# Both output projections of the mixer and of the cross attention in seven products of half-size blocks, their weight operands prepared and stored during the first FFN

## The chip, the core and the metric

The kernel runs on one core of a Trainium2 chip. TensorE multiplies matrices into PSUM, VectorE and ScalarE work element by element, GpSimd does small steps, and SyncE (SP in the profile) issues the DMAs. Each engine runs its own instructions in order; semaphores order them between engines. The time is device microseconds of one execution, the median of several runs.

## The reference

A decoder layer on x with T = 1024 tokens and D = 1024 features, in fp32:

```python
h = _layer_norm(ALPHA * h + 0.5 * _swiglu(h, ffn1_w_gate, ffn1_w_up, ffn1_w_down), ln1_g, ln1_b)
mix = _token_mixers(h, w_in, ..., w_out)             # concat([o_a, o_b]) @ w_out
h = _layer_norm(ALPHA * h + mix, ln2_g, ln2_b)
xa = _memory_cross_attention(h, mem, ..., xa_w_o)    # o.reshape(T, D) @ xa_w_o
h = _layer_norm(ALPHA * h + xa, ln3_g, ln3_b)
h = _layer_norm(ALPHA * h + 0.5 * _swiglu(h, ffn2_w_gate, ffn2_w_up, ffn2_w_down), ln4_g, ln4_b)
```

The FFNs have 2816 hidden features. The mixers are a gated linear recurrence with 4 heads of 128 (its normed and gated output is o_a, 512 features) and a spatial gating unit (o_b, 512 features). The cross attention has 4 heads of 256 and 256 memory tokens. The two products with w_out and xa_w_o, each 1024 x 1024 x 1024, are the output projections spoken of here.

## The kernel before

**Products.** Every fp32 operand is split into two fp32r tiles, hi = a rounded copy (ScalarE, L109) and lo = the operand less hi (VectorE, L110). `mm3` (L130) then makes one product of three matmuls, hi hi (L131), lo hi (L132) and hi lo (L133), each 128x128 by 128x512 into one PSUM bank. Activations are kept transposed (feature by token) in the tiles xh and xl, two halves of 512 tokens each, in eight k-tiles of 128 features.

**Stages.** In order: FFN 1; the mixers, first half of the tokens, then the second; the first output projection with LN2 (names acc_mx, wd_mx, r_mx); the cross attention, whose query projection (paq, weights waq) takes the normed tokens; the second output projection with LN3 (acc_xa, wd_xa, r_xa); FFN 2. The FFNs already use Winograd's form of Strassen's product, seven products of half-size blocks where the plain way has eight: gate and up (st_gf, st_uf) over 11 pairs of feature tiles, 7 products of 12 matmuls for each, and the down projection (dp_f).

**An output projection** is `down_group` (L226), called for the groups of token tiles (0, 1), (2, 3, 4) and (5, 6, 7). For every group the eight row blocks of the weights are loaded (512 KB each, SP's queue), split, and multiplied with the group's tiles, two PSUM banks a tile: 8 x 8 x 2 x 3 = 384 matmuls over the three groups, and 24 loads with 24 splits. Behind each group `residual_norm` (L214) runs for each of its tiles as a coroutine: it loads the residual, adds the accumulators on VectorE (L220), normalizes (L191 to L204), stores, and after a lag transposes the tile on TensorE (L158) back into xh and xl.

**What sets the order.** Coroutines are started with `spawn`, and `tick(us)` lets them go on when so many us of matrix products have been issued since. Tiles come from pools: `gpool` with 22 tiles of 4 KB a partition, `wpool` with 3 raw, 6 hi and 5 lo tiles for weights, and PSUM with 6 banks for products and 2 for transposes. A tile waits until the last reader of the buffer it takes has finished, and an engine that waits holds up what stands behind it on the same engine; SP issues all DMAs here, so a load that waits for a buffer holds up the loads and stores behind it. In the mixers `m1.tail()` is the last part of the second half: its four gate products (ps_wg, 48 matmuls each) and, by coroutine, the gating and the transposes of o (pt_oa). Group (0, 1) of the first projection, tokens of the first half, is run ahead of it (its residuals and norms fall into it), the other groups behind it. The query projection then starts with half 0, and the groups of the second projection run in the same manner, the first one inside the loop over the heads of half 1. FFN 2 starts with its first pair of feature tiles (pg_f).

Of the kernel before, what the change touches and what calls it, by code (L numbers as in the profile page):

```python
# [33 lines left out]
def hybrid_layer_kernel(ctx: ExitStack, tc: tile.TileContext, a, out):  # L34
# [29 lines left out]
    # Work that follows a matrix product on other engines runs as a coroutine: where the tensor  # L64
    # engine would wait for it, it yields the time of other products (in us) to issue first.
# [26 lines left out]
    # the tensor engine's clock rises while it works: transposes until the first tile is there  # L92
# [9 lines left out]
    # left and right operands of the products of the FFNs' down projection, by pair of feature tiles  # L102
    lops = dram.tile([7, NF // 2, P, HALF], F32, name="lops")
    rops = dram.tile([2, NF // 2, P, HALF], F32, name="rops")
    res = [dram.tile([T, D], F32, name=f"res{i}") for i in range(3)]

# [23 lines left out]
    def mm3(ps, lh, ll, rh, rl, first, last):  # L130
        nc.tensor.matmul(ps, lh, rh, start=first, stop=False)  # L131
        nc.tensor.matmul(ps, lh, rl, start=False, stop=False)  # L132
        nc.tensor.matmul(ps, ll, rh, start=False, stop=last)  # L133
# [73 lines left out]
    def layer_norm(y, gb, bb, name):  # L207
        """y: [P, 1024] tile, normalized over its free dim in place."""
# [5 lines left out]
    def residual_norm(tt, lag, acc, res_src, gb, bb, dst, name, keep=None):  # L214
        """dst = LN(alpha * res_src + acc) for a token tile, and its transpose."""
        r = gt(f"r_{name}")
        nc.sync.dma_start(r, res_src[tt * P:(tt + 1) * P, :])
        for dh in range(2):
            sl = slice(dh * 512, (dh + 1) * 512)
            nc.vector.scalar_tensor_tensor(r[:, sl], r[:, sl], ALPHA, acc[dh], op0=ALU.mult, op1=ALU.add)  # L220
        layer_norm(r, gb, bb, name)
        nc.sync.dma_start(dst[tt * P:(tt + 1) * P, :], r)
        yield lag
        yield from to_xT_steps(r, tt, list(range(KT)), name, keep, 2.6)
# [982 lines left out]
```

## Time and profile before

| | |
|---|---|
| Time, median of 3 runs (lowest, highest) | 2041.24 us (2035.83, 2042.89) |
| Span of the profiled execution | 2032.8 us |
| First and last start of st_gf (FFN 1 and FFN 2 together) | 62.7 and 1780.4 us |
| Gate products of the mixers (ps_wg), last start | 1082.5 us |
| First output projection (acc_mx), first and last start | 1022.2 and 1152.6 us |
| Query projection (paq), first and last start | 1152.8 and 1265.4 us |
| Second output projection (acc_xa), first and last start | 1275.2 and 1386.2 us |
| First gate product of FFN 2 (pg_f), start | 1386.5 us |

All but the first row are of one profiled execution, whose span is a little shorter than the time of the runs. Names are those of the tiles; a matmul counted as 0.39 us in the profile overlaps the next one. The profile's rows on which the argument rests are shown in the prediction, beside what is read from them.

### The profile page before, as it was taken

The page shows a single profiled execution, that of the slowest core. Times are in us where ns is not written, and L with a number is a line of the kernel's source. Part 1 is how long each engine was busy: PE and PEld are TensorE (multiplying, and loading weights), DVE is VectorE, ACT ScalarE, POOL GpSimd, SP SyncE. Part 2 cuts the span into 40 slices and gives each one's busy share as a digit, 9 for nine tenths or more (in the row PEclk, how much of TensorE's full clock was granted, in tenths as well). Part 3 has the DMA queues.
Part 4 walks back from the last instruction along what each step waited for, and adds up shares of the span by engine and source line. Part 5 has one row for each costly group of instructions (what it writes and reads, how often), then busy time and mean ns, then how long its engine had stood idle before and what let it go on. Part 6 is the DMA issues. An engine that isn't in the chain of part 4 may idle for free.

```text
span 2032.8 us, 25339 instructions
## 1 busy us (share of the span) xinstructions
PE 2015.5 (99%) x9646; PEld 1689.1 (83%) x9646; DVE 1504.1 (74%) x2246; ACT 890.0 (44%) x1239; POOL 102.5 (5%) x144
## 2 busy tenths in 40 slices
PE   8999999999999999999999999999999999999998
PEld 7888888888888888888888888888888888888886
DVE  5987677677668967948796855678776776776688
ACT  6633333334533467547644344444333333344432
POOL 0000000000002010100110100010000000000021
PEclk8999999999999999999999999999999999999999
DMA  8333233237887632123156522353232332378874
GB/s 263 122 114 119 78 114 119 78 119 250 290 289 261 222 116 73 53 63 105 41 176 228 162 88 74 122 197 119 88 126 82 104 127 81 109 249 291 297 254 172
DMA packets 244250, 306.88 MB, mean 151 GB/s; under 512 B 14368, under 2 KB 154272, under 8 KB 244128
## 3 DMA queue, kind: packets, MB, share of 16 engines
q1 hardware_dynamic: 244128, 305.26, 45.3%
q8 instruction: 76, 1.25, 0.2%
q14 instruction: 46, 0.38, 0.1%
HBM read 234.44 MB, written 70.78 MB: 150 GB/s over the span
## 4 chain that ended last, share of the span: by engine, by line
PE 93%; DVE 3%; DMA 2%; POOL 1%; issue 1%; SPq 0%; ACT 0%; POOLq 0%; DVEq 0%; ACTq 0%
PE st_gf L131 7%; PE st_uf L131 7%; PE st_gf L133 7%; PE st_uf L133 7%; PE st_gf L132 7%; PE st_uf L132 7%; PE dp_f L133 6%; PE dp_f L131 6%; PE dp_f L132 6%; PE psl L939 2%; PE acc_xa L131 1%; PE acc_xa L133 1%; PE acc_xa L132 1%; PE paq L131 1%; PE paq L133 1%; PE paq L132 1%
## 5 line engine op out<-in xcount | busy, mean ns | idle before, releaser
L132 PE MATMUL dp_f<-wd_f_l,ah_f 128*128 128x512 f32 x552 | 213.3, 390 | 0.0
L131 PE MATMUL dp_f<-wd_f_h,ah_f 128*128 128x512 f32 x552 | 208.4, 390 | 0.0
L133 PE MATMUL dp_f<-wd_f_h,al_f 128*128 128x512 f32 x552 | 206.1, 390 | 0.1
L133 PEld LDWEIGHTS dp_f<-wd_f_h,al_f 128*128 128x128 f32 x552 | 103.7, 188 | 22.2 <-DVE al_f L110 0.9
L132 PEld LDWEIGHTS dp_f<-wd_f_l,ah_f 128*128 128x128 f32 x552 | 103.6, 188 | 21.6
L131 PEld LDWEIGHTS dp_f<-wd_f_h,ah_f 128*128 128x128 f32 x552 | 103.6, 188 | 21.2
L109 ACT ACTIVATE wd_f_h<-wd_f_r 128x1024 fp32r<-128x1024 f32 x72 | 73.2, 1022 | 97.7 <-DVE wd_f_r L436 28.3
L110 DVE TENSOR_TENSOR al_f<-ar_f,ah_f 128x1024 fp32r<-128x1024 f32 x72 | 84.5, 1174 | 24.5 <-ACT ah_f L109 23.6
L109 ACT ACTIVATE ah_f<-ar_f 128x1024 fp32r<-128x1024 f32 x72 | 73.3, 1019 | 59.2 <-DMA ar_f<-lops 54.3
L110 DVE TENSOR_TENSOR wd_f_l<-wd_f_r,wd_f_h 128x1024 fp32r<-128x1024 f32 x72 | 84.3, 1175 | 12.5 <-ACT wd_f_h L109 12.2
L316 DVE TENSOR_TENSOR top_uf<-bot_uf,st_uf 128x512 f32<-128x512 f32 x21 | 14.4, 686 | 81.8 <-PE st_uf L133 81.8
L315 ACT ACTIVATE bot_gf<-st_gf 128x512 f32<-128x512 f32 x21 | 12.5, 597 | 137.1 <-PE st_gf L133 137.1
L560 POOL TENSOR_SCALAR nm_f<-nm_f 128x1 f32<-128x1 f32 x8 | 10.7, 1336 | 1198.8 <-ACT xl L559 1198.8
L131 PE MATMUL st_gf<-xh,wg_f_h 128*128 128x512 f32 x168 | 65.4, 389 | 0.0
L133 PE MATMUL st_gf<-xh,wg_f_l 128*128 128x512 f32 x168 | 65.4, 389 | 0.0
L131 PE MATMUL st_uf<-xh,wu_f_h 128*128 128x512 f32 x168 | 65.4, 389 | 0.0
L132 PE MATMUL st_uf<-xl,wu_f_h 128*128 128x512 f32 x168 | 65.4, 389 | 0.0
L133 PE MATMUL st_uf<-xh,wu_f_l 128*128 128x512 f32 x168 | 65.4, 389 | 0.0
L132 PE MATMUL st_gf<-xl,wg_f_h 128*128 128x512 f32 x168 | 65.3, 389 | 0.0
L109 ACT ACTIVATE wg_f_h<-wg_f_r 128x1024 fp32r<-128x1024 f32 x44 | 46.4, 1056 | 36.2 <-PE st_gf L132 29.3
L109 ACT ACTIVATE wu_f_h<-wu_f_r 128x1024 fp32r<-128x1024 f32 x44 | 46.3, 1053 | 35.7 <-issue 27.2
L110 DVE TENSOR_TENSOR wu_f_l<-wu_f_r,wu_f_h 128x1024 fp32r<-128x1024 f32 x44 | 53.6, 1219 | 3.2 <-PE acc_xa L132 3.2
(456 smaller groups left out, 5960.1 us busy)
## 6 DMA issues: line engine op xcount, KB each, us to landing
ar_f<-lops SPq DMA_DIRECT2D x66, 512.0 KB, 5.0
wd_f_r<-in_ffn_w_down_dram SPq DMA_DIRECT2D x56, 512.0 KB, 4.8
wg_f_r<-in_ffn_w_gate_dram SPq DMA_DIRECT2D x44, 512.0 KB, 3.8
wu_f_r<-in_ffn_w_up_dram SPq DMA_DIRECT2D x44, 512.0 KB, 3.8
wd_mx_r<-in_w_out_dram SPq DMA_DIRECT2D x24, 512.0 KB, 3.6
wd_xa_r<-in_xa_w_o_dram SPq DMA_DIRECT2D x24, 512.0 KB, 3.5
lops<-bot_gf SPq DMA_DIRECT2D x21, 512.0 KB, 2.7
lops<-top_uf SPq DMA_DIRECT2D x21, 512.0 KB, 2.8
```

The lines of the kernel that those rows point to most:

```text
L109: order(nc.scalar.activation(hi, src, AF.Copy))
L110: order(nc.vector.tensor_tensor(lo, src, hi.bitcast(F32), op=ALU.subtract))
L131: nc.tensor.matmul(ps, lh, rh, start=first, stop=False)
L132: nc.tensor.matmul(ps, lh, rl, start=False, stop=False)
L133: nc.tensor.matmul(ps, ll, rh, start=False, stop=last)
L315: nc.scalar.activation(b0, product(1), AF.Copy)
L316: nc.vector.tensor_tensor(t0, b0, product(2), op=ALU.add)
L560: nc.gpsimd.tensor_scalar(nmean, nmean, -1.0 / D, None, op0=ALU.mult)
L939: nc.tensor.matmul(psl[:m, (i * NC2 + c) * 64:(i * NC2 + c + 1) * 64] .rearrange("p (n b) -> p n b", b=B), e[:, :m], blk(e, B)[:, :, 1, :] ...
```

## The change

Both projections are made of seven products in Winograd's form. The tokens (two halves), the 1024 features (two halves) and the output columns (two halves) form 2x2 blocks. A product is four token tiles by 512 columns, 4 k-tiles and three matmuls: 48 matmuls, so 7 x 48 = 336 for a projection.

**Weight operands.** The seven right operands of each projection are blocks of the weights and running sums of them. They are made once, in FFN 1, by the coroutine `prepare_square`, a step each 13 us of products, 28 steps in all (7 operands x 2 pairs of k-tiles x 2 projections). A step loads a block into the one tile `pre`, or adds a block to what is there with an accumulating DMA that GpSimd issues (16 of the 28); ScalarE makes hi and -hi; a second accumulating DMA adds the block to -hi, which gives lo; both are stored to DRAM (hi from SP, lo from GpSimd). `later` starts the coroutine behind the memory keys and values. The projections load their operands ready (`fetch`, sh and sl, 28 loads of 512 KB for each projection) and split nothing.

**Token operands.** These need differences of the attention or mixer outputs of the two halves. The transposed outputs of the first half are stored (oa, ao) and loaded again (mx_again, ao_again); VectorE subtracts, and the results take the places of xh and xl.

**Order.** The first projection has its products in the order 2, 1 (ahead of `m1.tail()`), then behind it 7, 4, 6, 5 and 3. Product 5 completes the tokens of half 1 (done5), product 3 those of half 0 (done3); the tokens of half 1 take their LN statistics on ScalarE and GpSimd, those of half 0 on VectorE. The query projection starts with half 1. The second projection runs 1 and 7 inside the loop over the heads of half 0, then 4, 6, 5, 2, 3.

The core of the diff (comments that it drops, and helpers that only rename, are left out):

```diff
...
+    SUMS = {1: ["11"], 5: ["11", "12"], 6: ["11", "12", "22"], 4: ["11", "12", "22", "21"],
+            2: ["21"], 3: ["22"], 7: ["22", "12"]}
+    def prepare_square(w, ops, name):
+        wv = w.rearrange("(kb n i p) (db d) -> kb n db p i d", kb=2, n=2, i=2, p=P, db=2)
+        for n in range(2):
+            raw = None
+            for p, blocks in SUMS.items():
+                b = wv[int(blocks[-1][0]) - 1, n, int(blocks[-1][1]) - 1]
+                if len(blocks) == 1:
+                    raw = wpool.tile([P, 2, HALF], F32, tag="pre", bufs=1, name=f"pre_{name}_{n}{p}")
+                    nc.sync.dma_start(raw, b)
+                else:
+                    nc.gpsimd.dma_start(raw, b, accum_op=ALU.add)
+                hi = wpool.tile([P, 2, HALF], F32R, tag="whi", bufs=6, name=f"ph_{name}_{n}{p}")
+                lo = wpool.tile([P, 2, HALF], F32R, tag="wlo", bufs=5, name=f"pl_{name}_{n}{p}")
+                nc.scalar.activation(hi, raw, AF.Copy)
+                nc.scalar.activation(lo, hi.bitcast(F32), AF.Copy, scale=-1.0)
+                nc.gpsimd.dma_start(lo, raw, accum_op=ALU.add)
+                nc.sync.dma_start(ops[p - 1, n, 0], hi.bitcast(F32))
+                nc.gpsimd.dma_start(ops[p - 1, n, 1], lo.bitcast(F32))
+                yield 13
+    class Square:
...
+        def fetch(self, *ps):
+            for p in ps:
+                self.right[p] = []
+                for n in range(2):
+                    hi = wpool.tile([P, 2, HALF], F32R, tag="whi", bufs=6, name=f"sh_{self.name}_{p}{n}")
+                    lo = wpool.tile([P, 2, HALF], F32R, tag="wlo", bufs=5, name=f"sl_{self.name}_{p}{n}")
+                    for i, t in enumerate((hi, lo)):
+                        nc.sync.dma_start(t.bitcast(F32), self.ops[p - 1, n, i])
+                    self.right[p].append((hi, lo))
...
+        def part(self, p, bank, half, k0, t, n, first):
+            ts = slice(t * P, (t + 1) * P)
+            rh, rl = self.right[p][n]
+            for i in range(2):
+                k = k0 + 2 * n + i
+                mm3(bank[t], xh[half][:, k, ts], xl[half][:, k, ts], rh[:, i, :], rl[:, i, :],
+                    first and n == 0 and i == 0, n == 1 and i == 1, not first)
+        def step(self, p, bank, half, k0, n, first=False):
+            for t in range(4):
+                self.part(p, bank, half, k0, t, n, first)
+            tick(5.4)
+        def tiles(self, p, bank, half, k0, done, first=False):
+            for t in range(4):
+                for n in range(2):
+                    self.part(p, bank, half, k0, t, n, first)
+                done(t)
+                tick(2.7)
...
+        def finish(self, x, p2=None):
+            f, g = self.f, self.g
+            self.fetch(6)
+            for t in range(4):
+                self.residual(self.bot, g, t)
+                self.onto(self.bot[t][:, 1], x[t], ALU.subtract, ALPHA)
+            self.step(4, x, g, 4, 0)
+            self.step(4, x, g, 4, 1)
+            s1, s4 = {}, {}
+            for n in range(2):
+                self.put(self.s[n], f, 0, n)
+            for n in range(2):
+                s1[n] = self.a1[0][n]
+                nc.vector.tensor_tensor(s1[n], s1[n], self.s[n], op=ALU.subtract)
+                self.put(s1[n], g, 0, n)
+            self.fetch(5)
+            for t in range(4):
+                self.onto(self.bot[t][:, 0], x[t], ALU.add, ALPHA)
+            y = self.bank("sy")
+            def done6(t):
+                self.onto(self.bot[t][:, 0], y[t], ALU.subtract)
+            self.tiles(6, y, f, 0, done6, True)
+            for n in range(2):
+                s4[n] = self.a1[1](n)
+                nc.vector.tensor_tensor(s4[n], s4[n], self.s[n], op=ALU.subtract)
+                self.put(s4[n], f, 0, n)
+            self.fetch(3)
+            self.junk = gt("junk_xa") if p2 is None else xl[f][:, 4:6, :].rearrange("p k t -> p (k t)")
+            def done5(t):
+                self.onto(self.bot[t][:, 1], y[t])
+                self.early.append(self.norm(self.bot[t], g, t, 8 + 2.5 * t))
+                spawn(self.early[-1])
+            self.tiles(5, y, g, 0, done5)
+            if p2 is None:
+                self.fetch(2)
+            for t in range(4):
+                if p2 is None:
+                    self.residual(self.top, f, t)
+                    self.onto(self.top[t][:, 0], self.p1[t], ALU.add, ALPHA)
+                    self.onto(self.top[t][:, 1], self.p1[t], ALU.subtract, ALPHA)
+            if p2 is None:
+                z = self.bank("sz")
+                def done2(t):
+                    self.onto(self.top[t][:, 0], z[t])
+                self.tiles(2, z, f, 4, done2, True)
+            def done3(t):
+                self.onto(self.top[t][:, 1], y[t])
+                spawn(self.norm(self.top[t], f, t, 8 + 2.5 * t))
+            self.tiles(3, y, f, 0, done3)
...
+        spawn(later())
+    def later():
+        yield 20
+        for n, w in (("mx", a["w_out"][0]), ("xa", a["xa_w_o"][0])):
+            yield from prepare_square(w, sq_ops[n], n)
...
-            to_xT(o, self.half * NC2 + i, [0, 1, 2, 3], f"oa{self.half}{i}")
...
+            if self.half:
+                for n in range(2):
+                    if i == 0:
+                        msq.s[n] = gt(f"s3_mx{n}", (P, 2, HALF))
+                        msq.a1[0][n] = mixed_again(0, n)
+                    nc.vector.tensor_tensor(msq.s[n][:, :, cs], msq.a1[0][n][:, :, cs],
+                                            ptv[:, 2 * n:2 * n + 2, :], op=ALU.subtract)
+                    if last:
+                        msq.put(msq.s[n], 1, 0, n)
+                        msq.put(self.u[n], 1, 4, n)
+                        nc.vector.tensor_tensor(msq.s[n], msq.s[n], self.u[n], op=ALU.add)
+                return
...
+                    nc.sync.dma_start(oa_dram[0, j], self.oa[j])
...
+    def mixed_again(j, n):
+        t = gt(f"mx_again{j}{n}", (P, 2, HALF))
+        nc.sync.dma_start(t, oa_dram[j, n])
+        return t
...
-    run(mix_group((0, 1)))
+    msq.fetch(2, 1)
+    x = msq.bank("sx2")
+    for n in range(2):
+        msq.step(2, x, 0, 4, n, True)
+    msq.p2 = msq.copies(x, "p2")
+    x = msq.bank("sx")
+    for n in range(2):
+        msq.step(1, x, 0, 0, n, True)
     play(m1.tail())
+    msq.fetch(7)
+    msq.gb, msq.bb = load_bc(a["ln2_g"][0], a["ln2_b"][0], "mx")
+    for t in range(4):
+        msq.residual(msq.top, 0, t)
+        msq.onto(msq.top[t][:, 0], msq.p2[t], ALU.add, ALPHA)
+        msq.onto(msq.top[t][:, 0], x[t])
+        msq.onto(msq.top[t][:, 1], x[t], ALU.subtract, ALPHA)
     drain()
-    run(mix_group((2, 3, 4)))
-    run(mix_group((5, 6, 7)))
-    # ---- cross attention ----
+    for n in range(2):
+        msq.step(7, x, 1, 0, n)
+    msq.fetch(4)
+    msq.finish(x, msq.p2)
+    F, G = 1, 0
...
-        q_proj(0, c)
+        q_proj(F, c)
...
+    sq.fetch(1)
+    x = sq.bank("sx")
     for h in range(H):
-        if h:
-            next(first)
-        probs_T(1, h)
+        probs_T(G, h)
+        if h == 0:
+            sq.a1[0].update({n: attended_again(n) for n in range(2)})
         if h < H - 1:
-            scores(1, h + 1)
+            scores(G, h + 1)
+        if h < 2:
+            sq.step(1, x, F, 0, h, True)
+        elif h == 2:
+            sq.p1 = sq.copies(x, "p1")
+            sq.step(7, x, G, 0, 0)
         else:
-            next(first)
-        next(first)
-        attend(1, h)
-    run(first)
-    run(out_group((2, 3, 4)))
-    run(out_group((5, 6, 7)))
-    # ---- FFN 2 ----
+            sq.step(7, x, G, 0, 1)
+        if h == 1:
+            sq.fetch(7)
+        if h == 2:
+            sq.fetch(4)
+            sq.gb, sq.bb = load_bc(a["ln3_g"][0], a["ln3_b"][0], "xa")
+        attend(G, h)
+    sq.finish(x)
```

Three places show how it moves instructions.

**TensorE behind the last gate product** of the mixers (ps_wg_3; pt_oa are the transposes of o; wd_mx, sh_mx and sl_mx are weight operands; sy_mx are the banks of product 6, sx_mx those of products 1, 7 and 4). Before, the engine has there:

```order
L132 MATMUL ps_wg_3_8737<-wg_l,xh_116 128x512
L133 MATMUL ps_wg_3_8737<-wg_h,xl_118 128x512
L131 MATMUL acc_mx_0_8797<-wd_mx_0_h,xh_115 128x512
L132 MATMUL acc_mx_0_8797<-wd_mx_0_l,xh_115 128x512
L133 MATMUL acc_mx_0_8797<-wd_mx_0_h,xl_117 128x512
L131 MATMUL acc_mx_1_8798<-wd_mx_0_h,xh_115 128x512
L132 MATMUL acc_mx_1_8798<-wd_mx_0_l,xh_115 128x512
L133 MATMUL acc_mx_1_8798<-wd_mx_0_h,xl_117 128x512
L131 MATMUL acc_mx_0_8799<-wd_mx_0_h,xh_115 128x512
L158 MATMUL pt_oa_0_8765<-ident,ot_7748 128x128 x4
L158 MATMUL pt_oa_0_8772<-ident,ot_7748 128x128 x4
L132 MATMUL acc_mx_0_8799<-wd_mx_0_l,xh_115 128x512
```

Now it has, from the last rows of the same gate product:

```order
L136 MATMUL ps_wg_3_8905<-wg_l,xh_116 128x512
L137 MATMUL ps_wg_3_8905<-wg_h,xl_118 128x512
L1038 MATMUL pt_oa_8933<-ident,ot_8002 128x128 x4
L1038 MATMUL pt_oa_8946<-ident,ot_8002 128x128 x4
L1038 MATMUL pt_oa_8953<-ident,ot_8005 128x128 x4
L1038 MATMUL pt_oa_8992<-ident,ot_8005 128x128 x4
L135 MATMUL sy_mx_9155<-sh_mx_9065,xh_115 128x512
L136 MATMUL sy_mx_9155<-sl_mx_9066,xh_115 128x512
L135 MATMUL sy_mx_9156<-sh_mx_9065,xh_115 128x512
L136 MATMUL sy_mx_9156<-sl_mx_9066,xh_115 128x512
L135 MATMUL sx_mx_8680<-sh_mx_8960,xh_116 128x512
L136 MATMUL sx_mx_8680<-sl_mx_8961,xh_116 128x512
```

The matmuls of the group (2, 3, 4) that stood between the last gate product and the transposes are gone: all four transposes follow at once, and behind them the first rows of products 6 and 7, whose token operands are made from them.

**SP's queue there.** oa is the stored output of the first half, res the residual, sq_mx the prepared operands. Before, from the last weights of the first group on:

```order
L118 DMA wd_mx_7_r<-in_w_out_dram 128x1024
L118 DMA wg_r<-in_w_in_dram 128x2x512 x3
L217 DMA r_mx_8538<-res_121 128x1024
L217 DMA r_mx_8554<-res_121 128x1024
L118 DMA wg_r<-in_w_in_dram 128x2x512
L118 DMA wd_mx_0_r<-in_w_out_dram 128x1024
L118 DMA wd_mx_1_r<-in_w_out_dram 128x1024
L118 DMA wd_mx_2_r<-in_w_out_dram 128x1024
L118 DMA wd_mx_3_r<-in_w_out_dram 128x1024
```

Now, from the operands of product 4 on (9065 to 9069 are product 6's):

```order
L268 DMA sh_mx_9057<-sq_mx 128x1024
L268 DMA sl_mx_9058<-sq_mx 128x1024
L268 DMA sh_mx_9061<-sq_mx 128x1024
L268 DMA sl_mx_9062<-sq_mx 128x1024
L268 DMA sh_mx_9065<-sq_mx 128x1024
L268 DMA sl_mx_9066<-sq_mx 128x1024
L1231 DMA mx_again_8939<-oa 128x1024
L268 DMA sh_mx_9069<-sq_mx 128x1024
L1231 DMA mx_again_8943<-oa 128x1024
L191 DMA g_mx<-in_ln_g_dram 128x1024
L192 DMA b_mx<-in_ln_b_dram 128x1024
L298 DMA r_mx<-res_125 128x1024 x8
```

The two loads of mx_again are now in a row with the loads of operands, behind most of them, and the residuals (r_mx) stand behind both.

**VectorE at the end of the first projection**, up to the query projection (xl is the lo part of the transposed tokens, 117 of half 0 and 118 of half 1; pt_mx are the transposes on TensorE; r_mx the tiles being normed; waq the query weights). Before, at the place where the first query weights are split:

```order
L110 TENSOR_TENSOR xl_117<-pt_mx_0_9097,xh_115 128x4x128
L110 TENSOR_TENSOR xl_117<-pt_mx_4_9128,xh_115 128x4x128
L202 SCALAR_TENSOR_TENSOR r_mx_9027<-r_mx_9027,mv_mx_9034,g_mx 128x1024
L110 TENSOR_TENSOR waq_0_l<-waq_0_r,waq_0_h 128x1024
L204 SCALAR_TENSOR_TENSOR r_mx_9027<-r_mx_9027,rs_mx_9036,b_mx 128x1024
L110 TENSOR_TENSOR waq_1_l<-waq_1_r,waq_1_h 128x1024
L110 TENSOR_TENSOR xl_117<-pt_mx_0_9135,xh_115 128x4x128
L110 TENSOR_TENSOR xl_117<-pt_mx_4_9166,xh_115 128x4x128
L110 TENSOR_TENSOR waq_2_l<-waq_2_r,waq_2_h 128x1024
L110 TENSOR_TENSOR xl_118<-pt_mx_0_9173,xh_116 128x4x128
L110 TENSOR_TENSOR xl_118<-pt_mx_4_9204,xh_116 128x4x128
L110 TENSOR_TENSOR waq_3_l<-waq_3_r,waq_3_h 128x1024
```

Now, from the addition of product 3's last bank on:

```order
L302 TENSOR_TENSOR r_mx<-r_mx,sy_mx_9158 128x512
L200 BN_AGGR mv_mx_9359<-st_mx_9356 128x2
L113 TENSOR_TENSOR xl_118<-pt_mx_0_9368,xh_116 128x4x128
L113 TENSOR_TENSOR xl_118<-pt_mx_4_9400,xh_116 128x4x128
L206 SCALAR_TENSOR_TENSOR r_mx<-r_mx,mv_mx_9359,g_mx 128x1024
L196 BN_STATS st_mx_9388<-r_mx 128x6 x2
L113 TENSOR_TENSOR xl_118<-pt_mx_0_9432,xh_116 128x4x128
L208 SCALAR_TENSOR_TENSOR r_mx<-r_mx,rs_mx_9361,b_mx 128x1024
L200 BN_AGGR mv_mx_9391<-st_mx_9388 128x2
L206 SCALAR_TENSOR_TENSOR r_mx<-r_mx,mv_mx_9391,g_mx 128x1024
L196 BN_STATS st_mx_9420<-r_mx 128x6 x2
L208 SCALAR_TENSOR_TENSOR r_mx<-r_mx,rs_mx_9393,b_mx 128x1024
```

The splits of the transposed tokens, which alternated with query weights and the last rows of the group before, now alternate with the scalings and statistics of the other half's tiles, and the query weights stand ahead of them.

More of the change, by code (lines that the diff above doesn't have):

```diff
@@ L212, in layer_norm @@
         ln_apply(y, stt, gb, bb, name)
[L214 to L224, printed above, removed]
@@ L1124, in attend @@
         pTh, pTl = pts[half, h]
+        n = h % 2
+        if half == F:
+            ao = gt(f"ao{h}", (P, 2, HALF))
+        elif h < 2:
+            sq.s[n] = gt(f"s3_xa{n}", (P, 2, HALF))
         for j in range(2):
```

140 lines of the change are left out of this document (98 added, 42 removed).

## The prediction

> **What bounds the kernel now.** First the page: its span, and the engine that fills it.
>
> ```profile
> span 2032.8 us, 25339 instructions
> PE 2015.5 (99%) x9646; PEld 1689.1 (83%) x9646; DVE 1504.1 (74%) x2246; ACT 890.0 (44%) x1239; POOL 102.5 (5%) x144
> GB/s 263 122 114 119 78 114 119 78 119 250 290 289 261 222 116 73 53 63 105 41 176 228 162 88 74 122 197 119 88 126 82 104 127 81 109 249 291 297 254 172
> ```
>
> Then the waits of TensorE (total us, times, longest), longest and last of those that matter here:
>
> ```profile
> PE ptm L660 <- ACT mem L653: 3.3, 2, 2.2
> ...
> PE psl L939 <- DVE r_mx L220: 0.4, 1, 0.4
> ```
>
> Then busy time by stretch (sum and count for PE, PEld, DVE, ACT, POOL; granted clock, DMA share, GB/s): the start, first FFN, first output projection, second one.
>
> ```profile
> 10.00:15.00 5.00, 2.56 (x12) 1.86 (x12) 3.27 (x4) 2.99 (x4) 0.00 (x0) 0.64 1.08 380
> 15.00:20.00 5.00, 4.46 (x21) 4.26 (x21) 3.60 (x8) 2.21 (x3) 0.00 (x0) 0.50 1.07 366
> 20.00:25.00 5.00, 5.00 (x37) 5.00 (x36) 2.92 (x5) 0.63 (x1) 0.00 (x0) 0.83 1.12 317
> 200.00:250.00 50.00, 50.00 (x223) 41.39 (x222) 33.27 (x44) 16.09 (x20) 0.00 (x0) 1.00 0.28 90
> 1050.00:1100.00 50.00, 49.58 (x275) 42.61 (x275) 37.09 (x57) 21.69 (x42) 5.88 (x8) 1.00 0.53 197
> 1100.00:1150.00 50.00, 50.00 (x234) 41.58 (x233) 38.39 (x45) 20.95 (x23) 5.40 (x6) 1.00 0.60 196
> 1350.00:1400.00 50.00, 50.00 (x238) 41.56 (x237) 42.86 (x61) 18.77 (x38) 10.01 (x12) 1.00 0.54 182
> ```
>
> TensorE is the bound: after the start it waits 0.4 us in all. So matrix work that is removed is time gained, and every wait that is added on TensorE is time lost. Note VectorE in the stretches of the projections: 37 to 43 of 50 us. It has little room for a burst.
>
> **What is removed.** 50 us hold 222 to 223 matmuls of 512 columns; rows follow each other by 0.227 us (timeline: start, length, row), eight transposes take 0.8:
>
> ```profile
> 1093.15 0.39 PE L132 MATMUL acc_mx<-wd_mx_l,xh 128*128 128x512 f32 x1
> 1093.38 0.40 PE L133 MATMUL acc_mx<-wd_mx_h,xl 128*128 128x512 f32 x1
> 1093.61 1.04 PE L158 MATMUL pt_oa<-ident,ot 128*128 128x128 f32 x8
> 1094.40 0.70 PE L133 MATMUL acc_mx<-wd_mx_h,xl 128*128 128x512 f32 x2
> ```
>
> Each projection goes from 384 to 7 x 48 = 336 matmuls: 2 x 48 x 0.227 = **21.8 us gained**. One product (48) is 10.9 us, one of its four tiles 2.7. That 48 splits on ScalarE and VectorE go too is worth nothing by itself: neither was waited for.
>
> **Durations for the rest** (groups, mean ns; the last three rows min/median/max), and two rows of the timeline where VectorE works without a pause:
>
> ```profile
> L110 DVE TENSOR_TENSOR waq_l<-waq_r,waq_h 128x1024 fp32r<-128x1024 f32 x16 | 19.6, 1224 | 27.8 <-PE paq L133 22.7 <-PE acc_mx L132 2.6 <-issue 2.5
> L202 DVE SCALAR_TENSOR_TENSOR r_mx<-r_mx,mv_mx,g_mx 128x1024 f32<-128x1024 f32 x8 | 10.2, 1279 | 0.1
> L192 DVE BATCH_NORM_STATS2 st_mx<-r_mx 128x6 f32<-128x512 f32 x16 | 10.5, 683 | 0.0
> L220 DVE SCALAR_TENSOR_TENSOR r_mx<-r_mx,acc_mx 128x512 f32<-128x512 f32 x16 | 10.3, 678 | 0.0
> L913 DVE TENSOR_TENSOR e<-bs 128x256 f32<-128x256 f32 x56 | 23.4, 417 | 0.0
> L109 ACT ACTIVATE waq_h<-waq_r 128x1024 fp32r<-128x1024 f32 x16 | 17.0, 1063 | 45.0 <-PE paq L132 19.4 <-issue 14.1 <-PE acc_mx L133 8.1
> L182 POOL TENSOR_TENSOR rs_mx<-ve_mx,mhalf 128x1 f32<-128x1 f32 x8 | 6.4, 802 | 0.7
> L559 ACT ACTIVATE xl<-dt_f x8: 1038/1054/1065, 639.2 to 1976.9; 128x1024 fp32r<-128x1024 f32 x8
> L561 ACT ACTIVATE xl<-dt_f,nm_f x8: 1136/1152/1157, 641.2 to 1979.5; 128x1024 fp32r<-128x1024 f32 x8
> L560 POOL TENSOR_SCALAR nm_f<-nm_f x8: 207/1003/3140, 640.4 to 1978.6; 128x1 f32<-128x1 f32 x8
> ```
>
> ```profile
> 1077.68 1.89 DVE L875 TENSOR_TENSOR ot<-ot,sg 128x512 f32<-128x512 f32 x3
> 1084.09 2.35 DVE L110 TENSOR_TENSOR xl<-ut,xh 128x1024 fp32r<-128x1024 f32 x2
> ```
>
> Three rows of 0.68 take 1.89 and two of 1.22 take 2.35: in a queue each costs 0.08 less than its length, so 0.60 (512 columns), 1.13 or 1.20 (1024) and 0.34 (256). I use these.
>
> **Gap A, behind the mixers.** Call T0 the end of the last gate product ps_wg_3. Before, TensorE went on with tiles 2 to 4 of the projection. Now the transposes of the last o follow at once and then product 7, whose operand is made from them. Two queues stand before it.
>
> ```profile
> wd_mx_r<-in_w_out_dram SPq DMA_DIRECT2D x24, 512.0 KB, 3.6
> lops<-bot_gf SPq DMA_DIRECT2D x21, 512.0 KB, 2.7
> wg_f_r<-in_ffn_w_gate_dram SPq DMA_DIRECT2D x44, 512.0 KB, 3.8
> ```
>
> First SP: mx_again (the stored half of o) stands behind seven loads of products 7, 4 and 6, each of which waits for a slot that a matmul of ps_wg_3 frees, the first 4.3 us (19 matmuls) before T0. mx_again's two tiles are the 8th and 10th, the residual tiles the 13th to 16th. At 380 GB/s (10 to 15 us) 512 KB take 1.4 us, at 291 (busiest slices) 1.8; I take 1.6. The first lands 3.6 after issue, T0 - 0.7, the tenth at T0 + 13.7. Then VectorE's eight subtractions (0.4 each) with the transposes between them until T0 + 16.5, ScalarE's split 1.1; from T0 + 17.6 five rows of 1.13 and four of 0.60 up to the one that frees product 7's first bank: T0 + 25.6; its other tiles at 30.3, 32.7 and 33.9. From T0 to 36.5, when no tile waits any more, TensorE has 16 transposes and 52 matmuls, 13.4 us: **23 us idle**. With mx_again there in time the chain starts at T0 + 2.7 (the last sg and its product): 12. At 1.8 us a load: 25.
>
> **Gap B, into the query projection.** Product 5 ends the tokens of half 1, product 3 those of half 0; then q_proj starts with half 1. Let U be the start of product 5. Before, q_proj began with tiles normed 32 matmul-filled us earlier. Now all eight norms fall on products 5 and 3, 22.6 us with eight transposes between, and VectorE has in its order, up to the split of tile 7's transposes: 25 rows of 512 columns, 14 scalings of 1024, 4 splits of query weights, 3 small ones. At queue cost 15.0 + 16.8 + 4.5 + 0.5 = 36.8 us, from U + 3.8, where it has made product 3's operands; half 0's tiles 0 to 2 stand ahead of tile 7. ScalarE's two sums (1.05 and 1.15, each with a 0.18 read) and POOL's three steps (1.0, 0.75, 0.8) hold it up by another 4: it is there at U + 44.7. TensorE has 4.9 us of transposes and first matmuls in between: 44.7 - 22.6 - 4.9 = **17 us idle**; 13 without those hold-ups, 24 at full lengths and POOL's slow step.
>
> **Gap C, into the second FFN.** The same, milder: products 2 and 3 cover half 0's norms. VectorE still has 37 rows from U + 32.4 (three norm rows, three splits of gate and up weights, 20 of 512 and 11 of 256 columns: 21.7 us), to U + 54.1; TensorE gets there at U + 48.3: **6 us idle**, between 2 and 12. Within the heads, P1 and P7 take the place of the old tiles and I find 0.7; ahead of ps_wg_3 the scores of the last head lose some cover, 1.3: together **2** (0 to 4).
>
> **The clock.** Behind the waits at the start the granted clock is 0.64, 0.50 and 0.83 in three stretches of 5 us: 5.2 us lost. Behind gaps B and C I put 2 each, **4** (0 to 10). The Trainium skill, "TensorE: Matmul & The Clock Gate", Part 1, has the clock halved after an idle window of about 3.4 us and restored after as long a busy one: it speaks against any change that opens gaps. By it 1.7 us would be lost at each, an estimate from that page; the sum would be nearly the same.
>
> **The preparation in the first FFN.** 28 times: two activations (2 x 1.06), an accumulating DMA for lo, its store, and (16 of 28) an accumulating DMA onto the one tile pre, which the next activation waits for; ScalarE works in order, so gate and up splits wait behind it. Nothing in this trace accumulates. One such DMA costs between a store's 2.7 and three plain passes, 11.4 (3 x 3.8). Seven iterations have 35 products, 94.5 us: 7 x 3.1 (with 1 us of issue) + 3 x 3.8 for plain loads + 11 accumulations fit up to 5.6 us each. I take 5 (a load plus most of a second pass): no cost, with the splits' lead as cover:
>
> ```profile
> 199.64 1.06 ACT L109 ACTIVATE wg_f_h<-wg_f_r 128x1024 fp32r<-128x1024 f32 x1 [1.60 <-PE st_gf L132]
> ...
> 227.06 0.60 ACT L315 ACTIVATE bot_gf<-st_gf 128x512 f32<-128x512 f32 x1 [7.28 <-PE st_gf L133]
> ```
>
> The split at 199.64 serves the product that ends at 227.06, some 24 us later; others lead by 14. Beyond 5.6 each us costs 44 over 28 iterations, less that 14 once. The skill's "DMA: Bandwidth & Descriptors", Anatomy of one DMA, has 2.0 us + bytes / 436e3, an estimate of 3.2 for one pass and 4.4 for two; by it the term is 0 as well.
>
> **Sum.** -21.8 + 23 + 17 + 6 + 2 + 4 + 0 = +30: a span of 2063. The runs shown (2035.83 to 2042.89, median 2041.24) lie 3 to 10 above the profiled span of 2032.8, the median 8.4: **2071 us**.
>
> **Rivals.**
> - The accumulating DMA is slow. At 7.6 us (two plain loads) 2.0 x 44 - 14 = 74 more: 2145; at 6.5, 26 more: 2097. For it: every accumulation hangs on the one before through one tile. Against: the share of DMA time there is 0.28. Chance 0.16.
> - The loads ahead of mx_again land in time, gap A is 12 and the others as said: 2060. This lies in the forecast's range; chance 0.15 of the 0.62.
> - Faster: VectorE's queue drains sooner than its lengths say. It decides below 21.8 us of idle time in all. If B and C vanish and A is 12, it is -21.8 + 14 = -8: 2033. For it: 58 us of splits leave VectorE in the two projections. Against: those rows sat in other places; the norms' rows are the same ones, in a third of the time. Chance 0.12.
> - No change, idle time about equal to the gain (A 12, B 8): 2041. Chance 0.10.
>
> **Range and chances.** Forecast 0.62, slow accumulation 0.16, faster 0.12, no change 0.10. All terms at their low ends give 2053, at their high ends 2102. For 8 in 10 the range takes in most of the no-change case (down to 2037) and the milder part of slow accumulation (0.10 of the 0.16, up to 2110); outside lie the faster case, 0.12, 0.02 of no change and 0.06. A measurement here can tell about 0.3% (6 us) from no change: faster 0.12, same 0.10, slower 0.78.
>
> **What would show it.** In the profile after: TensorE busy near 1994; three holes in its row, the widest behind the last ps_wg_3 with "<- DVE r_mx" and, before it, VectorE waiting for mx_again; a wait of paq or pt_mx for VectorE of some 17 us in pieces; one at FFN 2's first pg. DMA landings of the accumulations under 5.6 us, and no st_gf or st_uf wait in 100 to 450 us. Wrong if TensorE waits in the first FFN, or if the holes are under 22 us together.

## The result and the profile after

The changed kernel takes **2133.18 us** (median of 4 runs, 2131.09 to 2135.29), the kernel before, beside it, 2039.2 us (2035.83 to 2042.89): a ratio of 1.0462, 95% interval 1.0442 to 1.0482. The time is slower, as forecast, but above the range (2037 to 2110).

The page of the changed kernel: span, engines, and the queue of the DMAs that GpSimd issues.

```profile
span 2129.3 us, 25517 instructions
PE 2029.2 (95%) x9550; PEld 1688.8 (79%) x9550; DVE 1492.0 (70%) x2240; ACT 931.6 (44%) x1311; POOL 166.8 (8%) x224
q0 software_dynamic: 12416, 37.75, 7.9%
```

TensorE, busy for 99% before, now stands still for 100 us, and its 96 fewer matmuls did not make it less busy: a matmul at the lower clock counts as busy for longer (0.57 us and more in place of 0.39 in the timeline under "Clock" below). Its waits say where (total us, times, longest):

```profile
PE st_uf L135 <- DVE top_gf L467: 14.1, 3, 8.0
PE pt_oa L1038 <- DVE s_mx L1047: 11.6, 1, 11.6
PE pt_mx L162 <- DVE xl L113: 7.0, 2, 4.6
PE dp_f L135 <- ACT ah_f L112: 7.0, 2, 6.0
PE sy_mx L135 <- ACT xh L112: 6.2, 1, 6.2
PE st_gf L135 <- ACT wg_f_h L112: 5.5, 2, 2.9
PE pg_f L136 <- DVE xl L113: 4.8, 1, 4.8
PE pt_mx L162 <- DVE mv_mx L200: 4.1, 1, 4.1
...
PE sx_mx L135 <- DVE r_mx L304: 1.5, 1, 1.5
```

The rows of pt_oa, sy_mx, sx_mx, pt_mx and pg_f are the three holes of the prediction. The rows of st_uf and st_gf, and 6.0 of dp_f's 7.0 us, are in the first FFN, where it expected none. The stages, by the first and last starts of their matmuls, with the terms of the prediction that fall into each:

| Stage | before | after | difference | predicted |
|---|---|---|---|---|
| to the first down product of FFN 1 (dp_f) | 490.7 | 553.5 | **+62.8** | 0 |
| from there to the last gate product (ps_wg) | 591.6 | 592.4 | +0.8 | +1.3 |
| to the first query product (paq) | 70.5 | 99.4 | +28.9 | -10.9 + 23 + 17 + 2 = +31 |
| to the first gate product of FFN 2 (pg_f) | 233.7 | 225.9 | -7.8 | -10.9 + 0.7 = -10 |
| to the end of the span | 646.3 | 658.1 | +11.8 | 6 + 2 = +8 |
| span | 2032.8 | 2129.3 | +96.5 | +30 |

Without the first row, the stages add up to +33.7. Windows over the first FFN's gate and up products (sum of busy time and count for PE, PEld, DVE, ACT, POOL; granted clock, DMA share, GB/s), first of the changed kernel:

```profile
63.00:553.00 490.00, 447.65 (x1889) 363.17 (x1887) 321.74 (x415) 208.55 (x264) 60.62 (x72) 0.96 0.76 214
```

and of the kernel before:

```profile
63.00:491.00 428.00, 428.00 (x1894) 354.45 (x1893) 326.07 (x421) 160.04 (x209) 0.00 (x0) 1.00 0.34 112
```

The same matmuls take 490 us instead of 428: 42 us idle, and 490 x 0.04, some 20, at the lower clock.

**A step of the preparation.** Timeline of ScalarE (start, length, row, and the idle time before it with what ended it; ph is hi, pl begins as -hi):

```profile
210.25 1.06 ACT L239 ACTIVATE ph_mx<-pre_mx 128x1024 fp32r<-128x1024 f32 x1 [15.42 <-DMA pre_mx<-in_w_out_dram]
212.16 1.04 ACT L240 ACTIVATE pl_mx<-ph_mx 128x1024 fp32r<-128x1024 f32 x1
227.25 1.06 ACT L239 ACTIVATE ph_mx<-pre_mx 128x1024 fp32r<-128x1024 f32 x1 [6.12 <-DMA pre_mx<-in_w_out_dram]
...
257.21 1.06 ACT L239 ACTIVATE ph_mx<-pre_mx 128x1024 fp32r<-128x1024 f32 x1 [8.87 <-DMA pre_mx<-in_w_out_dram]
259.12 1.04 ACT L240 ACTIVATE pl_mx<-ph_mx 128x1024 fp32r<-128x1024 f32 x1
271.77 1.06 ACT L239 ACTIVATE ph_mx<-pre_mx 128x1024 fp32r<-128x1024 f32 x1 [4.61 <-DMA pre_mx<-in_w_out_dram]
```

and of GpSimd, which issues the accumulation onto lo (L241), the store of lo (L243) and the accumulation onto pre (L236):

```profile
213.55 0.92 POOL L241 DMA_DIRECT2D pl_mx<-pre_mx  x1 [11.38 <-ACT pl_mx L240]
219.01 0.57 POOL L243 DMA_DIRECT2D sq_mx<-pl_mx  x1 [4.53 <-DMA pl_mx<-pre_mx]
219.60 1.22 POOL L236 DMA_DIRECT2D pre_mx<-in_w_out_dram  x1
...
260.51 0.85 POOL L241 DMA_DIRECT2D pl_mx<-pre_mx  x1 [6.64 <-ACT pl_mx L240]
266.31 0.57 POOL L243 DMA_DIRECT2D sq_mx<-pl_mx  x1 [4.95 <-DMA pl_mx<-pre_mx]
```

The parts of a step follow each other. From 210.25: hi, a split of up weights between, -hi, then 5.5 us of accumulation onto lo, the issue of its store, 7.6 us of accumulation onto pre, and only then the next hi: 17.0 us. The step from 257.21 to 271.77, with a plain load, takes 14.6, as the load may overwrite pre only when lo's accumulation has read it. These are two of 28. By the starts of hi, from 78.6 to 514.5 us, the mean is 16.1 us: 18.1 for a step that ends with an accumulation onto pre, 13.3 for one that ends with a plain load. In TensorE's order a step has 13.5 us of products.

At the end of a step ScalarE stands at the next hi, with the gate and up splits behind it (waits up to 600 us; total, times, longest):

```profile
ACT ph_xa L239 <- DMA pre_xa<-in_xa_w_o_dram: 74.8, 11, 14.9
ACT ph_mx L239 <- DMA pre_mx<-in_w_out_dram: 69.3, 12, 15.4
...
DVE wg_f_l L113 <- ACT wg_f_h L112: 51.8, 9, 10.5
```

ScalarE waits 144 us for pre, and VectorE 51.8 us for splits of gate weights that come late from it, where it had no such wait before. The DMA issues of that stretch (count, KB, median us from issue to landing):

```profile
pl_mx<-pre_mx POOLq DMA_DIRECT2D x14, 512.0 KB, 5.0
...
pre_mx<-in_w_out_dram POOLq DMA_DIRECT2D x8, 512.0 KB, 7.9
pre_xa<-in_xa_w_o_dram POOLq DMA_DIRECT2D x8, 512.0 KB, 8.5
...
pre_mx<-in_w_out_dram SPq DMA_DIRECT2D x5, 512.0 KB, 4.2
```

Onto a tile from DRAM an accumulation took 7.9 and 8.5 us here, about twice the 4.2 of the plain load.

### The profile page after: what moved, and what is told of

Read it like the earlier page. It is cut to its first block, busy times and chain, and to the rows that moved or that the text cites. A ratio compares the mean times of both kernels' runs of the same rounds, so it can differ in the third digit from the quotient of the medians.

```text
span 2129.3 us, 25517 instructions
## 1 busy us (share of the span) xinstructions
PE 2029.2 (95%) x9550; PEld 1688.8 (79%) x9550; DVE 1492.0 (70%) x2240; ACT 931.6 (44%) x1311; POOL 166.8 (8%) x224
## 4 chain that ended last, share of the span: by engine, by line
PE 68%; DVE 3%; DMA 1%; issue 1%; POOL 0%; ACT 0%; POOLq 0%; SPq 0%; DVEq 0%; ACTq 0%
PE dp_f L135 6%; PE dp_f L136 6%; PE dp_f L137 6%; PE st_uf L136 3%; PE st_gf L136 3%; PE st_gf L137 3%; PE st_uf L137 3%; PE st_uf L135 3%; PE st_gf L135 3%; PE psl L1119 2%; PE paq L135 1%; PE paq L136 1%; PE paq L137 1%; PE sx_mx L135 1%; PE ps_wu L135 1%; PE sx_mx L136 1%
## 5 line engine op out<-in xcount | busy, mean ns | idle before, releaser
L113 DVE TENSOR_TENSOR wg_f_l<-wg_f_r,wg_f_h 128x1024 fp32r<-128x1024 f32 x44 | 53.6, 1219 | 56.0 <-ACT wg_f_h L112 52.7
L112 ACT ACTIVATE wg_f_h<-wg_f_r 128x1024 fp32r<-128x1024 f32 x44 | 46.2, 1051 | 28.9 <-PE st_gf L136 15.5
L135 PEld LDWEIGHTS st_uf<-xh,wu_f_h 128*128 128x128 f32 x168 | 33.3, 198 | 26.2 <-issue 14.5
```

The costliest lines, as they stand in the source:

```text
L112: order(nc.scalar.activation(hi, src, AF.Copy))
L113: order(nc.vector.tensor_tensor(lo, src, hi.bitcast(F32), op=ALU.subtract))
L135: nc.tensor.matmul(ps, lh, rh, start=first, stop=False, skip_group_check=more)
```

## The experiments

Theories on the first FFN's 62.8 us: (1) the chain of a step just shown; (2) a price of each accumulating DMA, wherever it stands; (3) the added traffic; (4) lo keeps one of five wlo tiles from the gate and up splits. For the projections: SP's queue and VectorE's queue, as predicted, against chains that are late in themselves.

### First: what in the preparation costs

**e1_copy**: only copies in place of the preparation.

```diff
+                for i in range(2):
+                    nc.sync.dma_start(ops[p - 1, n, i], b)
```

> Left out: the sums and the hi/lo parts of the weight operands; each of the 56 operand tiles is one plain copy of a weight block from DRAM to DRAM, still one step each 13 us of products, so the projections read, multiply and norm as in the changed kernel. Theory 1 (a step of the preparation is a chain of some 16 us through the one tile pre, ScalarE's and GpSimd's in-order queues, against 13.5 us of products; ScalarE hands the delay on to the gate and up products): the first down product starts at 491 to 494 us instead of 553.5, the span falls from 2129.3 by 60 to 65 to 2064 to 2070, and what is left against 2032.8 is the two projections, +31 to 37. Theory 2 (every accumulating DMA costs about 1.5 us wherever it stands, 63 us over 44): the same here. Theory 3 (what costs is the added DMA traffic of the preparation as such, some 70 MB): the copies keep about half the traffic, so about half of the delay stays, span about 2097.

Span 2155.0, outside what any theory expected, and it tells little. The copies depend on nothing, stand at 14 to 126 us in SP's queue, among the first weight loads, and take 13 us each: the first Strassen product starts at 153.7 us instead of 63. From there to the last one it is 395.5 us, as before (394.7), but by then all copies were issued.

**e2_dve**: sums and lo by VectorE, blocks by plain loads.

```diff
-                    nc.gpsimd.dma_start(raw, b, accum_op=ALU.add)
...
+                    nc.sync.dma_start(lo.bitcast(F32), b)
+                    nc.vector.tensor_tensor(raw, raw, lo.bitcast(F32), op=ALU.add)
-                nc.scalar.activation(hi, raw, AF.Copy)
-                nc.scalar.activation(lo, hi.bitcast(F32), AF.Copy, scale=-1.0)
-                nc.gpsimd.dma_start(lo, raw, accum_op=ALU.add)
+                split(raw, hi, lo)
```

Here `split` makes hi on ScalarE and lo, raw less hi, on VectorE.

> Same operands, no accumulating DMA: the block is loaded plainly into the tile that later takes lo, VectorE adds it to pre (16 times) and makes lo by subtraction (28 times), 44 rows of 1.22 us more on VectorE in 400 us, where it is busy 37 of 50 us. Theory 1: a step is then 4 (load) + 1.2 + 1.06 + 1.2 with the load ahead, under 13.5: first down product at 491 to 497 us, span 2064 to 2073, time about 2070. Theory 2: the same. Theory 3: nearly all of the delay stays, span over 2110.

**e3_lo_dve**: of these, the change of lo alone (the last four lines).

> Only lo is made by VectorE (no -hi on ScalarE, no accumulation onto lo); the 16 accumulations onto pre, measured at 7.9 to 8.5 us, stay. Theory 1: the step shortens by the 6 to 7 us of the accumulation onto lo, to some 12 us, under 13.5, so nearly the whole delay goes: first down product at 491 to 500 us, span 2064 to 2075. Theory 2: 16 of 44 accumulations, by their time 130 of 270 us, stay, and with them 23 to 30 us: first down product at 514 to 521 us, span 2089 to 2096.

**e4_sum_dve**: of these, the change of the sums alone (the first three lines).

> Only the sums in pre are made by VectorE from a plain load; the 28 accumulations onto lo, measured at 5.0 us, stay. Theory 1: a step is about 10 us, under 13.5, so nearly the whole delay goes: first down product at 491 to 500 us, span 2064 to 2075. Theory 2: 28 of 44 stay, by their time 140 of 270 us, and with them 33 to 40 us: first down product at 524 to 531 us, span 2099 to 2106.

The down product's first matmuls (count, ns, first and last start) in e2, e3 and e4:

```profile
L135 PE MATMUL dp_f<-wd_f_h,ah_f x276: 387/389/504, 491.0 to 709.8; 128*128 128x512 f32 x138
```

```profile
L135 PE MATMUL dp_f<-wd_f_h,ah_f x276: 387/389/500, 491.9 to 710.1; 128*128 128x512 f32 x138
```

```profile
L135 PE MATMUL dp_f<-wd_f_h,ah_f x276: 387/389/796, 549.7 to 766.2; 128*128 128x512 f32 x138
```

e2 has 2070.57 us (ratio to before 1.0168, 1.0145 to 1.0191; span 2067.1), e3 a span of 2072.4, e4 of 2124.8. Theory 3 falls: e2 loads and stores the same blocks. In e3 the 16 accumulations onto pre stay and cost under 2 us up to the down product; theory 2 wanted 23 or more. e4 was expected by neither theory: 59 of 62.8 us stay, and the mean step is again 16.1 us. Its own timeline (SP, VectorE and ScalarE) shows why my 10 us for its step was wrong:

```profile
216.75 0.37 SPq L238 DMA_DIRECT2D pl_mx<-in_w_out_dram  x1
...
220.42 1.23 DVE L239 TENSOR_TENSOR pre_mx<-pre_mx,pl_mx 128x1024 f32<-128x1024 f32 x1 [3.55 <-DMA pl_mx<-in_w_out_dram]
221.74 1.06 ACT L240 ACTIVATE ph_mx<-pre_mx 128x1024 fp32r<-128x1024 f32 x1 [3.77 <-DVE pre_mx L239]
```

The block lands in the next lo tile and was issued 4 us after lo's store had been issued; the hi before stood at 203.23, so this step took 18.5 us. It is a chain again, but theory 4 explained it as well, and so three runs followed.

### Second: the chain or the tiles, and the first hole

**e5_yield19**: the changed kernel, `yield 19` for `yield 13`.

> The changed kernel with its accumulating DMAs, a step of the preparation each 19 us of products instead of 13 (the last six steps so fall into the down product). Theory 1 (a step is a chain of some 16 us, and TensorE is held up because only 13.5 us of products stand in its order for each): 16 is under 19, the waits of st_gf and st_uf go, first down product at 491 to 500 us instead of 553.5, span 2066 to 2080. Theory 2 (each accumulation onto lo, which the run without it showed to be the cause, costs some 2 us wherever it stands): 22 of 28 steps are still in front, first down product at 530 to 545 us, span about 2120. Theory 4 (lo holds one of the five wlo tiles that the gate and up splits need, from -hi until its store has landed, some 12 us of each step): 12 of 19 in place of 12 of 16, so the delay shrinks by a third or less, first down product at 520 to 540 us.

**e6_own_lo**: the changed kernel with lo in its own buffer, and `gpool` one tile smaller.

```diff
-                lo = wpool.tile([P, 2, HALF], F32R, tag="wlo", bufs=5, ...)
+                lo = wpool.tile([P, 2, HALF], F32R, tag="plo", bufs=1, ...)
```

> The changed kernel with its accumulating DMAs, lo in a tile of its own (one buffer; gpool has 21 tiles instead of 22 to make room), so that the gate and up splits keep all five wlo tiles; the chain of a step stays as it is. Theory 1 (the chain): the delay stays, first down product at 540 to 560 us, span 2115 to 2140. Theory 4 (the missing wlo tile): the delay goes, first down product at 491 to 505 us, span 2064 to 2085.

**e7_dve_4lo**: e2 with `bufs=4` for wlo.

> The version with sums and lo by VectorE (span 2067.1, first down product at 491.0), with four wlo tiles instead of five everywhere. Theory 4: the missing tile brings much of the delay back, first down product over 510 us, span over 2085. Theory 1: FFN 1 is as with five, first down product at 491 to 497 us; span 2065 to 2080 (the two projections have the tile less too).

The same row in e5, e6 and e7:

```profile
L135 PE MATMUL dp_f<-wd_f_h,ah_f x276: 388/390/797, 491.1 to 760.0; 128*128 128x512 f32 x138
```

```profile
L135 PE MATMUL dp_f<-wd_f_h,ah_f x276: 387/389/795, 551.7 to 776.2; 128*128 128x512 f32 x138
```

```profile
L135 PE MATMUL dp_f<-wd_f_h,ah_f x276: 387/389/504, 498.6 to 717.9; 128*128 128x512 f32 x138
```

e5 decides: the same accumulations, spaced 19 us instead of 13, cost the gate and up products nothing. From 124 to 371 us its hi follow each other by 18.9 to 19.0 us, the slot, and up to the down product ScalarE waits 3.5 us for the DMAs onto pre, in place of 144. Theory 2 wanted the down product at 530 or later. e6 gives the tile back and the delay stays; its span, 2141.7, is 1.7 above what theory 1 expected, with one `gpool` tile less. e7 (span 2088.1) fits neither theory wholly: its down product is 7.6 us later than e2's, not 20, but the span is 21.0 longer, as theory 4 had it. The other 13.4 us lie behind the first down product, 9.3 of them up to the last gate product of the mixers. So a wlo tile less does cost time, but it is not what delays the first FFN. Theory 1 holds: **a chain of 16.1 us on the mean in a slot of 13.5**.

The span of e5 did not fall to the expected 2066 to 2080 (2120.1): the down product takes 269 us instead of 215, with seven steps in it. What waits there is

```profile
PE dp_f L135 <- ACT ah_f L112: 22.6, 10, 4.3
```

and the accumulations land later there (8.4 us onto lo, 9.8 onto pre). That the steps cause all 54 us was not tried apart.

**g1_again_early**: e2 with mx_again(0) loaded ahead of `m1.tail()`.

```diff
-                        msq.a1[0][n] = mixed_again(0, n)
+    msq.a1[0].update({n: mixed_again(0, n) for n in range(2)})
     play(m1.tail())
```

> The version with sums and lo by VectorE, and the two loads of mx_again(0) issued ahead of the last gate products instead of behind seven operand loads. If those loads behind others in SP's queue cause the widest hole, as the prediction had it: the wait of pt_oa for s_mx falls from 12.1 us to 0 to 4, the wait of sy_mx for xh stays at 4 to 7, and the span falls from 2067.1 to 2056 to 2061. Rival (VectorE's chain behind them sets the end anyway): the wait only moves on to sx_mx and sy_mx, span 2064 to 2069.

Span 2054.5, 12.6 less than e2 and a little below the expected 2056 to 2061. TensorE's wait at the first hole in e2:

```profile
PE pt_oa L1037 <- DVE s_mx L1046: 12.1, 1, 12.1
```

and its waits at the three holes in g1:

```profile
PE pt_mx L162 <- DVE xl L113: 7.6, 3, 4.7
PE sy_mx L135 <- ACT xh L112: 6.2, 1, 6.2
PE pg_f L136 <- DVE xl L113: 4.1, 1, 4.1
PE pt_mx L162 <- issue: 3.7, 1, 3.7
...
PE pt_oa L1037 <- DVE ot L1031: 1.8, 1, 1.8
...
PE pt_oa L1037 <- DVE s_mx L1045: 0.7, 1, 0.7
```

The wait of pt_oa for s_mx went from 12.1 us to 0.7; 1.8 us for o itself came in its place. The two loads behind seven others were the larger part of the first hole.

### Third: VectorE's queue

**h1_late_norm**: g1 with `done3` only adding; the norms of half 0 follow once half 1 is transposed.

```diff
-                spawn(self.norm(self.top[t], f, t, 8 + 2.5 * t))
+                if not (p2 is not None):
+                    spawn(self.norm(self.top[t], f, t, 8 + 2.5 * t))
...
+            if p2 is not None:
+                for t in range(4):
+                    spawn(self.norm(self.top[t], f, t, 8 + 2.5 * t))
```

> The version with VectorE's sums and the early mx_again (span 2054.5), and of the first projection the norms of half 0 issued behind the transposes of half 1 instead of with product 3's tiles. If the second hole is VectorE's queue, as the prediction had it (half 0's rows stand ahead of what the query projection waits for): the waits of pt_mx, 11.3 us together, fall to 0 to 4 and the clock loss behind them goes too, span 2041 to 2047. Rival (the eight norms are late in themselves, since products 5 and 3 last only 22 us): the waits stay over 7 us, span 2050 to 2055, or half 0's norms come too late for its query products.

**g7_late_norm**: h1, with the residual sums of products 2 and 1 ahead of `m1.tail()` and without the wait of half 1's transposes for the last gate product.

> h1 and two more steps for the first hole: the sums of products 2 and 1 with the residual are made ahead of the last gate products, not behind them, and the transposes of o of half 1 do not wait for the fourth gate product. Expected: the wait of sx_mx for r_mx (1.1 us) goes, that of sy_mx for xh (6.2 us) falls to 3 to 6, span 1 to 5 us below h1, 2037 to 2045, so about the time of the kernel before.

**g8_late_both**: g7 with late norms in the second projection too.

> g7 with the late norms in the second projection too. If the third hole (pg_f for xl, 4.1 us) is the same queue: it goes, span 4 to 6 below g7. Rival (FFN 2 needs the tokens of half 1 only 11 us behind those of half 0, and VectorE's 16 us of their norms now come too late): a wait of the same size or longer, span from 1 below to 6 above g7.

**i1_query_lo_dma**: g7, lo of six query weights by -hi and an accumulating DMA.

> g7 (time 2047.8, span 2044.6), with lo of the first six query weights by the change's own means, -hi on ScalarE and an accumulating DMA, here where no step waits for it. It takes six rows of 1.22 us off VectorE, five of which stand ahead of the last transposes of half 1. If the second hole is VectorE's queue: the waits of pt_mx (7.1 us) fall by 5 to 6, span 2036 to 2041. Rival (GpSimd, in order, holds its small steps of the norms back behind these DMAs' waits, or ScalarE's six rows more do): the waits stay or grow, span 2043 to 2055.

| Run | waits of pt_mx | wait of sy_mx | waits of pg_f | span | ratio to before (interval) |
|---|---|---|---|---|---|
| g1 | 11.3 | 6.2 | 4.1 | 2054.5 | one run |
| h1 | 6.8 | 6.2 | 4.0 | 2051.1 | one run |
| g7 | 7.1 | none | 5.5 | 2044.6 | 1.0049 (1.0033 to 1.0064) |
| g8 | 7.0 | none | 5.3 | 2046.9 | 1.0069 (1.0052 to 1.0085) |
| i1 | 5.4 | none | 4.2 | 2045.0 | 1.0037 (1.0022 to 1.0052) |

What is left of pt_mx's waits in h1:

```profile
PE pt_mx L162 <- DVE xl L113: 6.8, 3, 4.7
```

h1 missed its expectation (0 to 4 us of waits, span 2041 to 2047); its span lies where the rival had it. It takes 4.5 of 11.3 us off, so half 0's rows were part of the second hole, but not the whole: VectorE is still busy without a pause there, with half 1's own norms and the splits of query weights among its rows. In g7 the wait of sy_mx goes, where 3 to 6 us were expected to stay; sx_mx waits 1.6 us for xh and ps_wg 1.1 us in its place, and the span falls by 6.5, more than expected. g8 brings nothing, as its rival had it: in the third hole two waits (3.3 and 2.0 us) take the place of one of 5.5. i1 shortens pt_mx by 1.7 us, not 5 to 6, and its gain over g7 is within the intervals; what holds the last transposes after that was not settled. No version beats the kernel before. The best, i1, is 0.37% above it, with 87 us of the changed kernel's loss undone (2045.8 against 2133.18).

## Why the prediction was wrong, and where it was right

**The step that failed** is the term for the preparation, "11 accumulations fit up to 5.6 us each. I take 5 ... no cost": put at 0, it came to 62.8 us. The mechanism it named (the next activation waits for the one tile pre, ScalarE works in order, the splits wait behind it) is what the trace and e5 show; the sizes were wrong. First the DMAs: onto lo an accumulation landed in 5.0 us, onto pre in 7.9 to 8.5, a mean of (28 x 5.0 + 16 x 8.2) / 44 = 6.16. By the prediction's own price that is 44 x 0.56 - 14 = 11. The larger part is the rest of the step. With the measured landings its budget for seven steps, of 3.1 us beside the DMAs each and 3.8 for a plain load, gives 4 x (3.1 + 5.0 + 8.2) + 3 x (3.1 + 5.0 + 3.8) = 101 us; seven steps of the measured 16.1 take 113, where 94.5 stood against them. 2.6 us late in each of 28 steps, less the 14 us of lead, is 59, near the 62.8. The timeline shows what the budget left out or made too small: issues of 0.9, 0.6 and 1.2 us on GpSimd, a split between hi and -hi, and a load that starts only when lo's accumulation is over (5.5 us from there to the next hi). How the 12 us divide among them was not measured. Its own sign of being wrong, TensorE waiting in the first FFN, was there.

The rival "slow accumulation" had this mechanism, with a chance of 0.16. The time came out between its two prices (2097 at 6.5 us, 2145 at 7.6), but not by its reason alone: at 6.16 us it gives 2082. In the sum for the range, the high ends of the terms as they stand add up to 2094, not 2102; no end of them reaches 2133.

**Removed work**: right. 96 matmuls fewer; the stage of the second projection, with under 2 us of waits, is 7.8 us shorter where 10.9 less 0.7 was expected.

**First hole**: mechanism right, shown by g1; 19.3 us of waits (11.6 + 6.2 + 1.5) for 23. The loads of mx_again hold VectorE's subtractions up (waits of VectorE; then count, ns, first and last start of the subtractions):

```profile
DVE s_mx L1047 <- DMA mx_again<-oa: 8.4, 2, 6.7
...
L1047 DVE TENSOR_TENSOR s_mx<-mx_again,pt_oa x8: 414/418/422, 1156.2 to 1161.5; 128x256 f32<-128x256 f32 x8
```

The last gate product ends at 1146.6, the prediction's T0. The second tile of mx_again, expected at T0 + 13.7, was there at T0 + 12.0, and product 7, expected at T0 + 25.6, began at T0 + 24.4. One sign was wrong: the widest wait is for s_mx, not for r_mx (1.5 us), as the transposes wait too. The rival "the loads land in time" put 11 us on those loads; g1 gained 12.6.

**Second hole**: 11.8 us of waits (7.0 + 4.1 + 0.7) for 17; VectorE's backlog is shown in part by h1, the rest is open. **Third**: 4.8 for 6. The stage behind it lost 11.8 where 8 was expected: 4.8, then 2.0 of waits in the second down product, and about 3.5 by the clock (0.93 in the 50 us from 1471, where it was 1.00 before); the rest is open.

**Clock**: it was put behind holes two and three alone, 4 us. It is lower behind the first as well; TensorE's timeline there:

```profile
1170.97 0.80 PE L135 MATMUL sx_mx<-sh_mx,xh 128*128 128x512 f32 x1 [1.51 <-DVE r_mx L304]
...
1175.40 0.57 PE L136 MATMUL sx_mx<-sl_mx,xh 128*128 128x512 f32 x1
1175.81 0.39 PE L137 MATMUL sx_mx<-sh_mx,xl 128*128 128x512 f32 x1
1176.04 0.39 PE L137 MATMUL sy_mx<-sh_mx,xl 128*128 128x512 f32 x1
```

Eleven matmuls behind the wait take 4.84 us, and the next follow by 0.23: 4.84 - 11 x 0.227 = 2.3 us lost. (Four matmuls ahead of that wait, from 1167.38 on, are as slow.) In windows of the same stage (granted clock third from the end):

```profile
1171.00:1196.00 25.00, 25.00 (x100) 20.48 (x101) 20.64 (x25) 6.26 (x6) 0.00 (x0) 0.90 0.59 214
1196.00:1246.00 50.00, 38.23 (x175) 31.30 (x174) 42.63 (x54) 22.23 (x33) 14.15 (x18) 0.88 0.48 160
```

The stage lost 28.9 + 10.9 = 39.8 us, of which waits are 31.1; 8.7 are left, and the clock (0.10 of 25 us and up to 0.12 of 50) is the only loss seen there. The Trainium skill, "TensorE: Matmul & The Clock Gate", Part 1, has half the clock until some 3.4 us of sustained work have passed; the trace agrees in kind, with 4.84 us in the place of 3.4, and 8.4 if it is counted from 1167.38, over a wait of 1.5 us. Over the whole program the sum of the projections' terms, +30, met +33.7, and e2, where the preparation delays nothing, has a span of 2067.1 for the forecast's 2063. That this comes so close is in part luck, as waits were over-rated and the clock under-rated.

## What to carry to other kernels

A preparation hidden behind matrix products is a second pipeline with a period: add up one round of it, with issue times, the wait for each landing and every reuse of its buffer, and hold it against the work that TensorE has per round; averages of engines and DMA share do not show it. An in-order engine that waits for such a round passes the delay on to everything behind it (ScalarE: 144 us of waits for pre, the weight splits behind it), so let a step wait only for what came long before, or do the small sums on the engine that has room (here VectorE: 0.3 us in that stage). A Strassen product saves one matmul in eight; here two loads behind seven others cost 12.6 us, more than one projection saves.

## What was not expected of the hardware

A 512 KB accumulation from DRAM took 7.9 to 8.5 us where the plain load took 4.2, and 9.8 in the down product of e5; from one tile to another in SBUF 5.0. The 512 KB copies from DRAM to DRAM in e1 took 13 us each from issue to landing, with 56 of them issued some 2 us apart.
